# Two heads side by side in the products of an attention pipeline: half the accumulators, one more step of lag

## The chip, the cores and the metric

The kernel runs on one core of a Trainium2 chip. The metric is the device time of one execution in microseconds (us), the median of the runs shown. The engines are TensorE (PE in the profile, with its weight loads as PEld), VectorE (DVE), ScalarE (ACT), GpSimd (POOL) and SyncE (SP, which issues most DMAs).

## What is computed

Two transformer blocks over 512 tokens of width 1024. The first block has two layers of attention with an MLP behind each; the second has attention and a mixture of experts. The change touches the attention of the first block's second layer alone. It has 16 heads in two groups of 8 (a group shares keys and values), head width 64, and three branches whose outputs are gated and added:

```python
def block(args):                       # one block of 128 queries
    i, qb, gb = args
    ...
    p_c = masked_softmax(s_c, cmp_end[None, :] <= t[:, None])    # compressed keys (31 of them)
    o_c = jnp.einsum('bghqn,bngd->bqghd', p_c.astype(vc.dtype), vc)
    ...                                # selection of key blocks
    p_s = masked_softmax(s_s, valid_s[:, :, None]).astype(v_g.dtype)
    o_s = jnp.einsum('bghqk,bgqkd->bqghd', p_s, v_g)             # selected keys
    ...
    p_w = masked_softmax(s_w, valid_w).astype(vw.dtype)
    o_w = jnp.einsum('bghqk,bkgd->bqghd', p_w, vw)               # window
    out = gb[..., 0:1] * o_c + gb[..., 1:2] * o_s + gb[..., 2:3] * o_w
```

With 512 tokens there are 8 blocks of 64 keys and up to 16 may be selected, and the window is 512 wide: the selected and the window branch both attend causally to all keys, each with its own keys and values.

## The kernel before

`layer_1` projects queries, keys and values, makes the compressed keys and their probabilities (`pcT`, transposed and gated), and then runs a software pipeline (`Pipeline`) over items. A step of the pipeline emits one operation of each of several items: an item's operation with lag 5 is emitted five steps after the item's first one. Within a step the order is that of the list `SM1`. Each engine works off its own instructions in the order in which they were emitted, and waits where an operand is not there yet.

An item is one softmax over up to 512 columns: one branch of one head, and one query block of four (`i` = 3, 512 keys) or two (`i` = 2 and 0, or `i` = 1 of both branches). Its operations are `qk` (products with the keys on PE, into a bank of PSUM), `max` (DVE, with the mask), `exp` (ACT), `norm` (the reciprocal on DVE, L618, and the scaling by it and the gate on POOL, L621), `T` (four transposes on PE into another bank, L626), `hi` (the copy of the transposed probabilities to an SBUF tile `PT`, L630, on ACT or DVE in turns), `pv` (the products with the values on PE, L1339) and `out` (the end of a pair of heads). Items come in rounds `f` = 0 to 7, one for each pair of heads, 10 items a round; four more items are for the compressed branch.

The values have 64 columns, so `halves_mm` issues its matmuls in pairs on the two column halves of PE (64 columns each). Before the change the halves are the two branches: the moving operand of a matmul is 256 columns, namely 128 queries of both heads, and the products of four items are emitted together in the step of the fourth. The compressed branch is added by `started`. Two PSUM banks hold the sums of a round; their halves still have to be added together, which `ended` does: for each head and bank a copy of one half by ACT (L1358), and an addition of the other by DVE (L1359) into the SBUF tile `om`; then the split into `oh` (ACT, L1360, rounded to fp32r) and `ol` (DVE, L1361, the rest).

The first nine steps of the pipeline run between the matmuls of the last projection (`q_half(1)`); all others run alone (`attend.run`), but for the last step, which runs within the output projection (`out_proj`, L347).

Of the kernel before, what the change touches and what calls it, by code (L numbers as in the profile page):

```python
# [9 lines left out]
F32 = mybir.dt.float32  # L10
# [3 lines left out]
ALU = mybir.AluOpType  # L14
# [4 lines left out]
S = 512  # L19
# [5 lines left out]
PB = 4  # L25

SM0 = [('pv', 6), ('T', 4), ('max', 1), ('hi', 5), ('norm', 3), ('qk', 0), ('lo', 5), ('out', 7), ('exp', 2)]
SM1 = [('hi', 6), ('norm', 3), ('T', 5), ('max', 1), ('qk', 0), ('exp', 2), ('pv', 7), ('out', 8)]
CM = [('min', 2), ('sm', 3), ('qk', 1), ('out', 6), ('T', 5), ('sc', 0)]
DA = [('qk1', 0), ('hi', 6), ('pv', 7), ('max1', 1), ('T', 5), ('join', 4), ('scale', 3), ('lo', 6), ('exp1', 1)]  # L30
DA0 = [('max0', 1), ('qk0', 0), ('exp0', 2)]
# [55 lines left out]
def tile_kernel(ctx: ExitStack, tc: tile.TileContext, I, out, stage=None, start=None):  # L87
# [11 lines left out]
    def ps(rows=128, cols=512):  # L99
        t = psum.tile([128, 512], F32, tag="ps", name="ps")  # L100
        return t[:rows, :cols]
# [486 lines left out]
    def softmax_item(sched, segs, qk, in1, v, out, ended, gate, parts=None):  # L588


        st = {}
        n = len(segs)
        at, w = [], 0
        for _, i in segs:
            at.append(slice(w, w + (i + 1) * 128))
            w += (i + 1) * 128

        def s_qk():
            st["s"] = ps(128, w)
            qk(st["s"], [(h, i, a) for (h, i), a in zip(segs, at)])  # L600

        def s_max():
            st["nm"] = att.tile([128, 2], F32, tag="nm", name="nm", bufs=4)
            st["p"] = att.tile([128, S], F32, tag="P", name="P", bufs=PBUF)
            for c, ((h, i), a) in enumerate(zip(segs, at)):
                nc.vector.tensor_tensor_reduce(st["p"][:, a], st["s"][:, a], in1(h, i), 1.0, 3e38, ALU.add, ALU.min,  # L606
                                               st["nm"][:, c:c + 1])

        def s_exp():
            st["sm"] = att.tile([128, 2], F32, tag="sm", name="sm", bufs=4)  # L610
            for c, a in enumerate(at):
                p = st["p"][:, a]
                nc.scalar.activation(p, p, AF.Exp, scale=-1.0, bias=st["nm"][:, c:c + 1],  # L613
                                     accum_out=st["sm"][:, c:c + 1])

        def s_norm():
            sm = st["sm"]
            nc.vector.reciprocal(sm[:, :n], sm[:, :n])  # L618
            for c, ((h, i), a) in enumerate(zip(segs, at)):
                p = st["p"][:, a]  # L620
                nc.gpsimd.tensor_scalar(p, p, sm[:, c:c + 1], 1.0 if gate is None else gate(h, i), op0=ALU.mult, op1=ALU.mult)  # L621

        def s_T():
            st["t"] = ps(128, w)
            for j in range(0, w, 128):
                nc.tensor.transpose(st["t"][:, j:j + 128], st["p"][:, j:j + 128], ident)  # L626

        def s_hi():
            if parts:
                (nc.vector.tensor_copy if parts[3] else nc.scalar.copy)(parts[0]()[:, :w], st["t"])  # L630
                return
            st["h"], st["l"] = (att.tile([128, S], F32R, tag="PT" + c, name="PT" + c, bufs=3) for c in "hl")
            nc.scalar.activation(st["h"][:, :w], st["t"], AF.Copy)

        def s_lo():
            if not parts:
                nc.vector.tensor_tensor(st["l"][:, :w], st["t"], st["h"][:, :w], ALU.subtract)

        def s_pv():
            if parts:  # L640
                return parts[1]()
            for (h, i), a in zip(segs, at):
                o, empty, use = out(h)
                pv([(h, i)], [a], o(), v, st["h"], st["l"], empty, use is not None)

        def s_out():
            if parts:
                return parts[2]()
            for h in sorted(ended):
                o, _, use = out(h)  # L650
                if use:
                    use(o())

        fs = dict(pv=s_pv, T=s_T, qk=s_qk, hi=s_hi, max=s_max, exp=s_exp, norm=s_norm, lo=s_lo, out=s_out)
        return [(lag, fs[n]) for n, lag in sched]
# [26 lines left out]
    def lazy(f):  # L682
        box = []

        def get():
            if not box:
                box.append(f())
            return box[0]
        return get
# [151 lines left out]
    def hslice(h):  # L841
        return slice(h % 2 * 64, h % 2 * 64 + 64)
# [247 lines left out]
    def layer_1():  # L1090
# [184 lines left out]
        def scores_T(g, half):  # L1275

            p = ps()
            for h in range(4):
                for n in range(2):
                    nc.tensor.matmul(p, kcs[g][n][:, 96 - h * 32:224 - h * 32], qst[g * 8 + half * 4 + h],  # L1280
                                     start=h == 0 and n == 0, stop=h == 3 and n == 1)
            tag, bufs = ("t4", T4) if g else ("PT", 4)
            scT[g, half] = att.tile([128, S], F32, tag=tag, name="sc", bufs=bufs)
            nc.scalar.activation(scT[g, half], p, AF.Copy)

# [46 lines left out]

        def halves_mm(o, of, start=False, stop=False):
            for c in range(2):
                dst, v, p = of(c)
                nc.tensor.matmul(dst(o[c * 64:c * 64 + 64]), v, p, start=start, stop=stop, skip_group_check=True,  # L1339
                                 tile_position=(0, c * 64))  # L1340

        def started(f):
            o = [ps(), ps()]
            for b in range(2):
                halves_mm(o[b], lambda a: (lambda z: z.rearrange("p (i a n) -> p i a n", i=2, a=2)[:, :, a],
                                           vcs[f // 4][:, f % 2 * 2 + a],
                                           pcT[:, f // 2, b * 256:b * 256 + 256].rearrange("p (i n) -> p i n", i=2)), start=True)
            return o

        def ended(f, o):  # L1350

            y = att.tile([128, S], F32, tag="om", name="om", bufs=1)
            for a in range(2):
                hs = hslice(a)
                for b in range(2):
                    v = o[b].rearrange("p (i a n) -> p i a n", i=2, a=2)[:, :, a]
                    dst = y[hs, b * 256:b * 256 + 256].rearrange("p (i n) -> p i n", i=2)
                    nc.scalar.activation(dst, v[64:128], AF.Copy)  # L1358
                    nc.vector.tensor_tensor(dst, v[0:64], dst, ALU.add)  # L1359
            nc.scalar.activation(oh[:, f], y, AF.Copy)  # L1360
            nc.vector.tensor_tensor(ol[:, f], y, oh[:, f], ALU.subtract)  # L1361

        def qk(s, segs):
            for n, i, a in segs:
# [1 line left out]
                for c in range(2):  # L1366
                    nc.tensor.matmul(s[:, a], qst[h][:, i * 128:w], kst[n % 2][h // 8][c][:, :w], start=c == 0, stop=c == 1)

        def both_pv(i, at, p, o, g):

            for j in range(i + 1):
                halves_mm(o[i // 2], lambda c: (lambda z: z[:, i % 2 * 256:i % 2 * 256 + 256], vsw[:, j, c * 2 + g],
                                                p[c][0][:, :, p[c][1] + at + j * 128:p[c][1] + at + j * 128 + 128]), stop=j == i)

        def pair_items(f):
            o = lazy(lambda: started(f))
            new = lambda: att.tile([128, 2, S], F32, tag="PT", name="PT", bufs=4)
            out = []

            def item(segs, place, take, use, n):  # L1380
                out.append(softmax_item(SM1, segs, qk, lambda n, i: cmask[:, 384 - i * 128:], None, None, None,
                                        lambda n, i: gate[:, i, n // 2 * 3 + 1 + n % 2:n // 2 * 3 + 2 + n % 2],
                                        (place, take, use, n % 2)))
            nothing = lambda: None
            for part in ((3,), (2, 0)):
                p = [lazy(new), lazy(new)]
                for b in range(2):
                    for a in range(2):
                        def take(p=p, part=part):
                            for i, at in zip(part, (0, 384)):  # L1390
                                both_pv(i, at, [(t(), 0) for t in p], o(), f // 4)
                        item([(4 * f + 2 * a + b, i) for i in part], lambda p=p, a=a, b=b: p[b]()[:, a],
                             take if a and b else nothing, nothing, a + b)
            p = lazy(new)
            for a in range(2):
                item([(4 * f + 2 * a, 1), (4 * f + 2 * a + 1, 1)], lambda a=a, p=p: p()[:, a],
                     (lambda p=p: both_pv(1, 0, [(p(), 0), (p(), 256)], o(), f // 4)) if a else nothing,
                     (lambda: ended(f, o())) if a else nothing, a)
            return out

        items = [cmp_item(0, 0), cmp_item(0, 2)]
# [933 lines left out]
```

## Time and profile before

| | |
|---|---|
| median of three runs | 2227.85 us (2227.54 to 2230.63) |
| profiled execution, its own time | 2226.52 us |
| its span in the profile | 2224.8 us |
| mean granted TensorE clock | 0.979 of full speed |
| busy: PE, DVE, ACT, POOL | 95%, 54%, 39%, 20% of the span |

The span runs from the first to the last instruction of the trace; the 1.7 us by which the execution is longer lie around it. Times in the rows below count from the span's start. The steps of the pipeline that run alone lie between some 815 and 977 us.

### The profile page before, as it was taken

The numbers are of one execution on the slowest core, as the hardware profiler recorded it, in microseconds if no ns is written. First come the engines' busy times: TensorE is split into PE (matmuls) and PEld (weight loads), VectorE is DVE, ScalarE is ACT, GpSimd is POOL, SyncE is SP. The second block draws the span as 40 slices with busy tenths as digits, with TensorE's granted clock in tenths as the row PEclk, the third lists the DMA queues.
The fourth block names the chain that finished last, engine by engine and source line by source line (L and its number), as shares of the span: only waits on it lengthen the run. The fifth ranks groups of instructions, "written<-read, shape, count | busy, mean of one in ns | idle before, by whom it ended". The sixth has DMA issues, their size and how long they took to land.

```text
span 2224.8 us, 29271 instructions
## 1 busy us (share of the span) xinstructions
PE 2110.3 (95%) x10935; PEld 1560.8 (70%) x10935; DVE 1192.2 (54%) x2417; ACT 859.4 (39%) x1656; POOL 437.7 (20%) x564
## 2 busy tenths in 40 slices
PE   7999999999999988999999999989888999999997
PEld 6877788888888776668888887777767444444443
DVE  5587654578675557644587686563655132222223
ACT  4524563344343356743344344463653110101000
POOL 4333240000001354531000001454363000000000
PEclk9999999999999999999999999999998999999999
DMA  4221022432313210012532312312016999999995
GB/s 132 68 76 48 1 75 70 160 123 76 114 57 103 84 39 1 1 39 76 170 113 82 119 48 78 102 36 77 29 31 240 372 409 409 409 409 409 409 408 207
DMA packets 118833, 328.62 MB, mean 148 GB/s; under 512 B 10604, under 2 KB 12716, under 8 KB 118688
## 3 DMA queue, kind: packets, MB, share of 16 engines
q1 hardware_dynamic: 115888, 318.87, 39.3%
q0 software_dynamic: 2800, 7.84, 1.1%
q8 instruction: 88, 1.44, 0.3%
q14 instruction: 57, 0.47, 0.1%
HBM read 324.49 MB, written 2.11 MB: 147 GB/s over the span
## 4 chain that ended last, share of the span: by engine, by line
PE 47%; DVE 4%; POOL 1%; ACT 1%; issue 1%; DMA 0%; DVEq 0%; POOLq 0%; ACTq 0%
PE ps L2034 15%; PE ps L404 10%; PE ps L347 8%; PE ps L743 5%; PE ps L2005 3%; PE ps L2101 2%; DVE sl L1740 1%; POOL sh L1736 1%; PE ps L318 0%; POOL wlo L280 0%; DVE w L1724 0%; DVE w L1732 0%; PE ps L319 0%; PE ps L317 0%; PE ps L2052 0%
## 5 line engine op out<-in xcount | busy, mean ns | idle before, releaser
L267 ACT ACTIVATE whi<-raw 128x1024 fp32r<-128x1024 f32 (+2 forms) x162 | 168.3, 1042 | 355.0 <-PE ps L404 153.2
L280 POOL TENSOR_TENSOR wlo<-raw,whi 128x512 fp32r<-128x512 f32 (+1 forms) x132 | 169.1, 1302 | 390.3 <-ACT whi L267 362.0
L2034 PE MATMUL ps<-ew,xt 128*64 128x512 f32 x1024 | 229.9, 597 | 0.0
L282 DVE TENSOR_TENSOR wlo<-raw,whi 128x1024 fp32r<-128x1024 f32 (+2 forms) x96 | 116.7, 1215 | 204.7 <-ACT whi L267 204.4
L404 PE MATMUL ps<-oTl,whi 128*128 128x512 f32 (+2 forms) x576 | 211.4, 371 | 1.4 <-DVE oTl L311 1.4
L404 PE MATMUL ps<-oTh,whi 128*128 128x512 f32 (+2 forms) x576 | 211.6, 371 | 0.5 <-ACT oTh L310 0.5
L404 PE MATMUL ps<-oTh,wlo 128*128 128x512 f32 (+2 forms) x576 | 166.6, 370 | 0.0
L2034 PEld LDWEIGHTS ps<-ew,xt 128*64 128x64 f32 x1024 | 69.4, 137 | 128.2 <-issue 120.1
L347 PE MATMUL ps<-whi,uTh 128*128 128x512 f32 (+2 forms) x384 | 152.6, 398 | 5.0 <-ACT uTh L310 2.9
L347 PE MATMUL ps<-whi,uTl 128*128 128x512 f32 (+2 forms) x384 | 148.5, 388 | 2.9 <-DVE uTl L311 2.9
L347 PE MATMUL ps<-wlo,uTh 128*128 128x512 f32 (+2 forms) x384 | 119.4, 390 | 6.4 <-POOL wlo L280 6.0
L404 PEld LDWEIGHTS ps<-oTl,whi 128*128 128x128 f32 x576 | 108.5, 188 | 20.8 <-DVE oTl L311 2.1
L404 PEld LDWEIGHTS ps<-oTh,whi 128*128 128x128 f32 x576 | 108.5, 188 | 19.8 <-ACT oTh L310 1.2
L2034 PE MATMUL ps<-ew,hid 128*64 128x512 f32 x512 | 118.4, 600 | 0.7 <-ACT hid L2054 0.7
L404 PEld LDWEIGHTS ps<-oTh,wlo 128*128 128x128 f32 x576 | 104.8, 188 | 18.8
L694 DVE TENSOR_TENSOR x<-ps,x 128x512 f32<-128x512 f32 x124 | 82.1, 686 | 66.5 <-PE ps L347 39.6
L445 POOL DMA_DIRECT2D room<-gains x5 | 2.9, 574 | 566.7 <-DVE fwlo L289 283.6
L613 ACT ACTIVATE P<-P,nm 128x512 f32<-128x512 f32 (+2 forms) x192 | 106.0, 554 | 14.0 <-DVE nm L606 13.0
L626 PE MATMUL ps<-cst,P 128*128 128x128 f32 x480 | 79.4, 289 | 22.1 <-POOL P L621 21.6
L2082 POOL CAST pick<-cst 32x128 fp32r<-32x128 f32 x16 | 4.9, 307 | 443.3 <-PE ps L2089 443.3
L2044 ACT ACTIVATE silu<-ps 128x512 f32<-128x512 f32 x16 | 9.6, 597 | 212.8 <-PE ps L2034 212.8
L347 PEld LDWEIGHTS ps<-wlo,uTh 128*128 128x128 f32 x384 | 73.3, 194 | 24.3 <-POOL wlo L280 10.8
(555 smaller groups left out, 5016.8 us busy)
## 6 DMA issues: line engine op xcount, KB each, us to landing
ew<-w SPq DMA_DIRECT2D x384, 512.0 KB, 10.2
raw<-mlp_w SPq DMA_DIRECT2D x80, 512.0 KB, 3.6
fraw<-mlp_w SPq DMA_DIRECT2D x48, 512.0 KB, 5.8
raw<-w_in SPq DMA_DIRECT2D x24, 512.0 KB, 3.9
raw<-ab_w_in SPq DMA_DIRECT2D x20, 512.0 KB, 3.5
raw<-c_w_in SPq DMA_DIRECT2D x12, 512.0 KB, 3.5
raw<-ab_w_out SPq DMA_DIRECT2D x8, 512.0 KB, 3.7
raw<-c_w_out SPq DMA_DIRECT2D x8, 512.0 KB, 3.7
```

What stands on the lines that cost most here:

```text
L267: nc.scalar.activation(hi[:, :w], raw[:, :w], AF.Copy)
L280: nc.gpsimd.tensor_tensor(lo[:, h], raws[r][:, h], hi[:, h], ALU.subtract)
L282: nc.vector.tensor_tensor(lo[:, :w], raws[r][:, :w], hi[:, :w], ALU.subtract)
L347: nc.tensor.matmul(p, a[:, tt], w[:, k], start=u == 0 and n == 0, stop=u == nk - 2 and n == 5)
L404: nc.tensor.matmul(p[:, tt], w[:, k, ff], b[:, u + k, tt], start=start and n == 0, stop=u == nk - 2 and n == 5, **kw)
L613: nc.scalar.activation(p, p, AF.Exp, scale=-1.0, bias=st["nm"][:, c:c + 1], accum_out=st["sm"][:, c:c + 1])
L626: nc.tensor.transpose(st["t"][:, j:j + 128], st["p"][:, j:j + 128], ident)
L694: nc.vector.tensor_tensor(xs, p, xs, ALU.add)
L743: nc.tensor.matmul(acc[b][t], p[:, 2 * h + k, tt], v[:, k], start=begins and h == 0 and m == 0, stop=m == 5, skip_group_check=True)
L2005: nc.tensor.matmul(v, htok[a][:, t, c * 128:(c + 1) * 128], oo[q][:, t], start=t == 0 and a == 0, stop=t == NT - 1 and a == 1)
L2034: nc.tensor.matmul(p[n][half(b)], xs[:, half(b)], w[b][:, n * 512:n * 512 + 512], start=k == 0, stop=k == nk - 1)
L2101: nc.tensor.matmul(p, ot[r][:, t * 128:(t + 1) * 128], ys[r][a][:, nn], start=j == 0 and a == 0, stop=j == len(rs) - 1 and a == 1)
```

## The change

- The two column halves are the two heads of the round, not the two branches. A matmul's moving operand is 128 queries of one head, so `both_pv` issues two pairs (one for each branch) of 128 columns where there was one pair of 256. The branches are added up by accumulation in one PSUM bank; `started` writes the compressed branch with one pair of 512 columns.
- `ended` has one ACT copy from that bank into `oh` and one DVE subtraction from that bank into `ol`; the tile `om` goes.
- An item pair (two heads, one branch) has its products two items earlier than the four together had: `take` is called at every second item.
- `PT` tiles are [128, 512], eight of them, where four of [128, 2, 512] were.
- In `SM1` the lag of `hi` is 7 (6 before), of `pv` 8 (7), of `out` 9 (8).

```diff
-SM1 = [('hi', 6), ('norm', 3), ('T', 5), ('max', 1), ('qk', 0), ('exp', 2), ('pv', 7), ('out', 8)]
+SM1 = [('hi', 7), ('norm', 3), ('T', 5), ('max', 1), ('qk', 0), ('exp', 2), ('pv', 8), ('out', 9)]
...
-        def halves_mm(o, of, start=False, stop=False):
+        def halves_mm(o, at, of, start=False, stop=False):
             for c in range(2):
-                dst, v, p = of(c)
-                nc.tensor.matmul(dst(o[c * 64:c * 64 + 64]), v, p, start=start, stop=stop, skip_group_check=True,
+                nc.tensor.matmul(o[c * 64:c * 64 + 64, at], *of(c), start=start, stop=stop, skip_group_check=True,
                                  tile_position=(0, c * 64))
...
         def started(f):
-            o = [ps(), ps()]
-            for b in range(2):
-                halves_mm(o[b], lambda a: (lambda z: z.rearrange("p (i a n) -> p i a n", i=2, a=2)[:, :, a],
-                                           vcs[f // 4][:, f % 2 * 2 + a],
-                                           pcT[:, f // 2, b * 256:b * 256 + 256].rearrange("p (i n) -> p i n", i=2)), start=True)
+            o = ps()
+            halves_mm(o, slice(0, S), lambda a: (vcs[f // 4][:, f % 2 * 2 + a], pcT[:, f // 2, :]), start=True)
             return o
...
         def ended(f, o):
-            y = att.tile([128, S], F32, tag="om", name="om", bufs=1)
-            for a in range(2):
-                hs = hslice(a)
-                for b in range(2):
-                    v = o[b].rearrange("p (i a n) -> p i a n", i=2, a=2)[:, :, a]
-                    dst = y[hs, b * 256:b * 256 + 256].rearrange("p (i n) -> p i n", i=2)
-                    nc.scalar.activation(dst, v[64:128], AF.Copy)
-                    nc.vector.tensor_tensor(dst, v[0:64], dst, ALU.add)
-            nc.scalar.activation(oh[:, f], y, AF.Copy)
-            nc.vector.tensor_tensor(ol[:, f], y, oh[:, f], ALU.subtract)
+            nc.scalar.activation(oh[:, f], o, AF.Copy)
+            nc.vector.tensor_tensor(ol[:, f], o, oh[:, f], ALU.subtract)
...
-        def both_pv(i, at, p, o, g):
+        def both_pv(i, at, b, p, o, g):
             for j in range(i + 1):
-                halves_mm(o[i // 2], lambda c: (lambda z: z[:, i % 2 * 256:i % 2 * 256 + 256], vsw[:, j, c * 2 + g],
-                                                p[c][0][:, :, p[c][1] + at + j * 128:p[c][1] + at + j * 128 + 128]), stop=j == i)
+                halves_mm(o, slice(i * 128, i * 128 + 128),
+                          lambda c: (vsw[:, j, b * 2 + g], p[c]()[:, at + j * 128:at + j * 128 + 128]), stop=j == i)
...
+            new = lambda: att.tile([128, S], F32, tag="PT", name="PT", bufs=8)
...
+            def items(segs, take, use=nothing):
+                p = [lazy(new), lazy(new)]
+                for a in range(2):
+                    out.append(softmax_item(SM1, segs(a), qk, lambda n, i: cmask[:, 384 - i * 128:], None, None, None,
+                                            lambda n, i: gate[:, i, n // 2 * 3 + 1 + n % 2:n // 2 * 3 + 2 + n % 2],
+                                            (p[a], (lambda: take(p)) if a else nothing, use if a else nothing, a)))
             for part in ((3,), (2, 0)):
                 for b in range(2):
+                    def take(p, part=part, b=b):
+                        for i, at in zip(part, (0, 384)):
+                            both_pv(i, at, b, p, o(), f // 4)
+                    items(lambda a, b=b, part=part: [(4 * f + 2 * a + b, i) for i in part], take)
+
+            def last(p):
+                for b in range(2):
+                    both_pv(1, 256 * b, b, p, o(), f // 4)
+            items(lambda a: [(4 * f + 2 * a, 1), (4 * f + 2 * a + 1, 1)], last, lambda: ended(f, o()))
```

## Rows read from the trace of the kernel before

**Rows 1.** The page: busy shares, and the chain by engine

```profile
PE 2110.3 (95%) x10935; PEld 1560.8 (70%) x10935; DVE 1192.2 (54%) x2417; ACT 859.4 (39%) x1656; POOL 437.7 (20%) x564
...
PE 47%; DVE 4%; POOL 1%; ACT 1%; issue 1%; DMA 0%; DVEq 0%; POOLq 0%; ACTq 0%
```

**Rows 2.** Busy us by stretch: length, PE PEld DVE ACT POOL; PEclk, DMA, GB/s

```profile
820.00:980.00 160.00, 142.65 (x990) 106.03 (x990) 106.45 (x408) 107.50 (x325) 76.27 (x126) 0.93 0.00 1
```

**Rows 3.** PE's waits from 822 to 872 us: in total, times, longest

```profile
PE ps L626 <- POOL P L621: 3.4, 2, 2.1
```

**Rows 4.** PE's waits from 884 to 970 us

```profile
PE ps L626 <- POOL P L621: 10.5, 5, 2.1
```

**Rows 5.** Timeline at the end of round 3: start, length (us), engine, instruction [idle before]

```profile
902.25 0.62 PE L626 MATMUL ps<-cst,P 128*128 128x128 f32 x4
...
903.33 1.08 PE L1339 MATMUL ps<-PT,vsw 128*64 128x256 f32 x8
...
904.35 0.66 PE L626 MATMUL ps<-cst,P 128*128 128x128 f32 x4
...
904.51 0.65 ACT L1358 ACTIVATE om<-ps 64x256 f32<-64x256 f32 x2
...
904.92 1.61 DVE L1359 TENSOR_TENSOR om<-ps,om 64x256 f32<-64x256 f32 x4 [0.23 <-ACT om L1358]
...
905.36 0.62 PE L626 MATMUL ps<-cst,P 128*128 128x128 f32 x4
...
906.30 0.60 PE L626 MATMUL ps<-cst,P 128*128 128x128 f32 x4
906.57 0.63 ACT L1360 ACTIVATE oTh<-om 128x512 fp32r<-128x512 f32 x1 [0.48 <-DVE om L1359]
...
907.23 0.69 DVE L1361 TENSOR_TENSOR oTl<-om,oTh 128x512 fp32r<-128x512 f32 x1 [0.70 <-ACT oTh L1360]
...
907.84 0.68 DVE L630 COPY PT<-ps 128x512 f32<-128x512 f32 x1
...
908.44 0.15 DVE L618 RECIPROCAL sm<-sm 128x2 f32<-128x2 f32 x1
...
908.79 1.73 POOL L621 TENSOR_SCALAR P<-P,sm,gate 128x384 f32<-128x384 f32 x3 [3.52 <-ACT PT L630]
...
909.51 0.86 PE L626 MATMUL ps<-cst,P 128*128 128x128 f32 x4 [2.13 <-POOL P L621]
```

**Rows 6.** Busy us by stretch, columns as in rows 2: where the clock was low, and one where not

```profile
863.00:866.40 3.40, 3.40 (x12) 2.32 (x12) 1.32 (x6) 1.45 (x6) 2.52 (x5) 0.61 0.00 0
...
890.40:893.60 3.20, 3.20 (x17) 2.29 (x18) 2.82 (x13) 3.20 (x13) 3.02 (x7) 0.60 0.01 3
894.00:907.00 13.00, 13.00 (x105) 10.33 (x102) 8.03 (x31) 8.35 (x24) 5.61 (x9) 1.00 0.01 2
910.90:914.10 3.20, 3.20 (x19) 1.77 (x20) 1.66 (x6) 2.57 (x10) 2.21 (x5) 0.60 0.00 0
...
931.40:934.50 3.10, 3.10 (x18) 1.58 (x14) 0.64 (x2) 1.54 (x6) 1.19 (x3) 0.59 0.00 0
...
969.00:972.00 3.00, 3.00 (x18) 1.49 (x15) 0.00 (x0) 0.60 (x4) 1.07 (x2) 0.59 0.00 0
```

**Rows 7.** Timeline: the products of four items, two records a matmul

```profile
899.36 1.95 PE L1339 MATMUL ps<-PT,vsw 128*64 128x256 f32 x16
```

**Rows 8.** Groups of instructions, 820 to 980 us: count, busy us, mean ns, idle before

```profile
L626 PE MATMUL ps<-cst,P 128*128 128x128 f32 x303 | 50.5, 289 | 16.4 <-POOL P L621 15.9
L1339 PE MATMUL ps<-PT,vsw 128*64 128x256 f32 x320 | 42.3, 407 | 0.0
...
L1339 PEld LDWEIGHTS ps<-PT,vsw 128*64 128x64 f32 x320 | 23.2, 146 | 12.9 <-issue 3.7
...
L1359 DVE TENSOR_TENSOR om<-ps,om 64x256 f32<-64x256 f32 x32 | 12.0, 412 | 4.9 <-ACT om L1358 4.0
...
L1358 ACT ACTIVATE om<-ps 64x256 f32<-64x256 f32 x32 | 10.9, 377 | 5.7 <-PE ps L1339 3.9 <-DVE om L1359 1.7
```

More of the change, by code (lines that the diff above doesn't have):

```diff
@@ L1281, in scores_T @@
                                      start=h == 0 and n == 0, stop=h == 3 and n == 1)
-            tag, bufs = ("t4", T4) if g else ("PT", 4)
+            tag, bufs = ("t4", T4) if g else ("PT", 8)
             scT[g, half] = att.tile([128, S], F32, tag=tag, name="sc", bufs=bufs)
@@ L1375, in pair_items @@
         def pair_items(f):
             o = lazy(lambda: started(f))
-            new = lambda: att.tile([128, 2, S], F32, tag="PT", name="PT", bufs=4)
+            new = lambda: att.tile([128, S], F32, tag="PT", name="PT", bufs=8)
             out = []
[L1380 to L1383, printed above, removed]
@@ L1385, in pair_items @@
             for part in ((3,), (2, 0)):
-                p = [lazy(new), lazy(new)]
                 for b in range(2):
[L1388 to L1398, printed above, removed]
+                    def take(p, part=part, b=b):
+                        for i, at in zip(part, (0, 384)):
+                            both_pv(i, at, b, p, o(), f // 4)
```

## The prediction

> **What bounds the kernel now.** Read the page first: PE is busy for 95% of the span, and the chain that ended last lies almost wholly on it [rows 1]. So only what PE does, or waits for, can move the time much; DVE and ACT count where PE waits for them. Next the stretch in which the pipeline runs alone [rows 2]. Of 160 us PE is busy for 142.65 at a mean granted clock of 0.93, DVE for 106.45, ACT for 107.50, POOL for 76.27; DMA does nothing. No engine is full there, so one looks for who holds up whom. PE's waits name one holder: the transposes L626 wait for POOL's scaling L621, twice between 822 and 872 us, 3.4 us in all, and five times between 884 and 970, 10.5 us [rows 3, 4]. That is seven waits, one for each of the rounds 0 to 6; the eighth round ends under the output projection.
>
> The timeline around one of them shows why [rows 5]. At 904.35 the products of the round are issued and the next transposes start. ACT copies halves of the banks from 904.51 on, DVE adds four times, ACT rounds at 906.57, and DVE's subtraction runs from 907.23 to 907.92. All of this is one chain to and fro between two engines in order, and behind it in DVE's queue stand a copy of PT (907.84) and a reciprocal (908.44). POOL, idle for 3.52 us, scales at 908.79, PE transposes at 909.51. Meanwhile PE had three short steps, with no products in them: transposes at 904.35, 905.36 and 906.30, 0.94 to 1.01 us a step, done about 907.3. The chain from 904.35 to 909.51 is 5.16 us long, the work that covers it about 3: PE stands for 2.13 us.
>
> The clock is the second cost. In five stretches of 3.0 to 3.4 us the granted clock averages 0.59 to 0.61, so 1.2 GHz most of the time, with PE busy throughout; the 13 us from 894 on, without a wait, are at 1.00 [rows 6]. Each of the five comes right behind one of the seven waits (two waits have none).
>
> **The change part by part.**
>
> *The end of a round.* Eight instructions of ACT and DVE on 64x256 go (four of 377 ns, four of 412 ns [rows 8]); the rounding and the subtraction stay (0.63 and 0.69 us [rows 5]), both now from PSUM. For the rounding from PSUM there is no row with this output; I take the 0.63. The chain behind the last product becomes 0.63 + 0.69 + 0.68 (copy of PT) + 0.15 (reciprocal) + 0.72 (scaling, 908.79 to 909.51), and about 0.6 for three handovers like the 0.2 from 908.59 to 908.79: 3.5 us instead of 5.16. Even under the old cover of 3 us PE would stand for 0.5 us, not 2.13.
>
> *Products at every second item.* The cover grows as well. Now the step after next behind a round's end holds the first products of the next round and its compressed branch: to the three steps (2.9 us) come eight records on two halves (0.88 us), the compressed branch (as much), and a switch (0.25, below): 4.9 us. The chain of 3.5 us is covered, and 1.4 us are to spare. So all seven waits go: -13.9 us (3.4 + 10.5). The least that this part can bring is seven times (2.13 - 0.5), some 11 us.
>
> *The clock behind the waits.* The five stretches are 15.9 us long; at full clock their work takes 0.6 of that: -6.4 us. If the clock stays as it is, 0; if the edges outside my stretches count, -8.
>
> *The products themselves.* A matmul is two records on each half. Eight pairs of records take 1.95 us [rows 7]; the last lasts 0.41, so a pair of 256 columns comes every (1.95 - 0.41) / 7 = 0.22 us. There are 160 pairs before (320 records [rows 8]) and 320 of 128 columns after. The nearest row for 128 columns is the transposes, four in 0.60 to 0.62 us with 0.29 for the last, so one every 0.11 us, its own weight load included [rows 5, 8]. Half of 0.22 is 0.11: the pairs cost as much together as before, 0. From above: if PE waited for the whole load of 146 ns [rows 8] with every pair, 320 x 0.036 = +12 us. I take 0, because the transposes load twice as many columns in the same 0.11. The compressed branch is one pair of 512 columns for two of 256: 0.
>
> *Switches between forms.* PE goes to its halves five times a round, not three times. A step with four pairs lasts from 902.25 to 904.35, 2.10 us; without products 0.97; four pairs are 0.88 [rows 5]. The rest, 0.25 us, is the price of going there and back. 8 rounds x 2 x 0.25 = +4.0 us. From below 0, if it hides. The Trainium skill, TensorEngine Tiling (Array Packing), Key Properties, speaks against the change here: changing the tiling mode drains the engine. The 0.25 us agree; without that rule the sum would be 4.0 us lower.
>
> *Copies and products a step later.* The copies stand first in ACT's and DVE's steps, so with a lag of 7 they no longer hold up the exponentials behind them until PE's transposes of one step before. The transposed bank is held one step longer, but the sums hold one bank instead of two: PSUM stays even. The eight PT tiles are as large together as the four. 0 in the sum. The pipeline has one step more; at its drain no instruction is added, the last products come behind the same last transposes, with 0.9 us of other products between: 0, at worst +1. No DMA and no POOL instruction is added, moved or passed by another.
>
> *Is there another bound behind PE?* With 16 us less, DVE has 106.45 - 12.0 and ACT 107.50 - 10.9 in 144 us [rows 2, 8]: 66 and 67%. No.
>
> **The sum.** -13.9 - 6.4 + 4.0 = -16.3 us. Against the profiled execution, 2226.52: 2210.2. The median of the runs is 1.3 above it, so I forecast 2211.5. What comes after is issued behind this stage and moves with it.
>
> **The rivals.**
>
> 1. *The clock does not recover* although the waits go. Of seven waits two were not followed by a low stretch, and long stretches without waits are at 1.00 [rows 6], so rather no. -13.9 + 4.0: 2218.
>
> 2. *Short pairs wait for their weights.* Twice as many loads for the same columns: +12, so 2223.7. Against it the transposes. The Trainium skill, TensorE: Matmul & The Clock Gate, Back-to-back issue gap, gives about 81 ns at 128 columns and 131 at 512 for bf16 streams of loads and matmuls, so few columns cost more each; the rows here (0.11 against 0.22) don't show it for fp32.
>
> 3. *PE keeps waiting at the round's end*, because the recurrence has another cause: DVE's reciprocal or the copies, now elsewhere in the order, are late again, and the clock falls behind it. Half the waits and no clock: -7 + 4.0, 2224.5.
>
> 4. *The two halves stop running side by side* with 128 columns, say for want of issue or because both heads load the same values: each pair takes 0.11 more. 320 x 0.11 = +35: 2246, slower. It decides from 16.3 / 320 = 0.05 us a pair on. Against it: a pair of 256 columns comes every 0.22 us, twice the 0.11 of a single transpose of 128, so the halves do run side by side before [rows 7], and nothing that made them is taken away.
>
> 5. *More than the sum*: the switches hide (-4.0) and the clock gives 8: 2206.
>
> **How the numbers follow.** What differs by under 0.2% (4.5 us) can hardly be told from no change. Chances: the forecast 0.58 (2208 to 2216), rival 1 0.13, rival 2 0.08, rival 3 0.08, rival 4 0.05, rival 5 0.08. Rivals 2 and 3 lie at the edge of what can be told (2223.4): half of their 0.16 counts as the same. Faster: 0.58 + 0.13 + 0.08 + 0.08 = 0.87; same 0.08; slower 0.05. The range runs from the gain of rival 5 with 2 us on its far side (2204) to rival 2 (2224); it leaves out rival 4 and parts of 2, 3 and 5.
>
> **What the profile after would show.** PE's transposes without the seven waits of 2 us; 640 records of 128 columns with a pair every 0.11 us; a mean clock of 0.98 or more in this stretch; the stretch of [rows 2] some 16 us shorter; one ACT and one DVE instruction at a round's end. Wrong would be: waits of PE for POOL as long as before, pairs at 0.15 us or more, low stretches without waits, or a new wait of PE for a PSUM bank (copies that come a step later free it later).

## The result, and the profile after

The changed kernel takes 2206.4 us (median of four runs, 2203.8 to 2209.3) where the kernel before takes 2229.2 beside it: ratio 0.9898, 95% interval 0.9881 to 0.9915, or 22.8 us less (19 to 27). Forecast were 2211.5 us, 16.3 less, in a range of 2204 to 2224, and faster with a chance of 0.87. The direction and the places are right; the size of two terms and the reason given for one are not.

The profiled execution took 2207.28 us. Its page, busy shares and the chain that ended last, to be held against [rows 1]:

```profile
PE 2105.7 (95%) x11223; PEld 1568.5 (71%) x11223; DVE 1179.3 (53%) x2385; ACT 847.9 (38%) x1624; POOL 439.1 (20%) x564
...
PE 55%; DVE 5%; POOL 2%; ACT 1%; issue 1%; DMA 0%; DVEq 0%; POOLq 0%; ACTq 0%
```

PE is about as busy in all, in 19 us less, and the chain still lies on it. The stretch from the first transpose behind the pipeline's fill to the output projection, in the kernel before and in the changed one (busy us by stretch: length, PE PEld DVE ACT POOL; PEclk, DMA, GB/s):

```profile
819.50:977.40 157.90, 140.54 (x980) 104.39 (x980) 105.45 (x405) 106.28 (x322) 76.65 (x127) 0.93 0.00 1
```

```profile
819.60:956.20 136.60, 134.28 (x1269) 110.94 (x1269) 94.50 (x378) 96.11 (x294) 77.35 (x128) 0.98 0.01 2
```

The stretch is 21.3 us shorter, which is the whole gain: it starts at the same time, and what lies behind it takes 1249.3 us instead of 1247.4 (between 1247 and 1252 in all profiles here but that of the experiment that works on other numbers). PE stands for 2.3 us in it (its length less PE's busy time), where it stood for 17.4. PE's waits of the changed kernel from 820 to 958 us, and from 878 to 957 alone:

```profile
PE ps L626 <- POOL P L621: 4.7, 2, 4.5
PE ps L1321 <- POOL cx L1315: 1.9, 2, 1.6
```

```profile
PE ps L626 <- POOL P L621: 0.2, 1, 0.2
```

The 4.5 us are the fill, just ahead of the stretch: the projection has ended, and the first softmaxes are not ready. The seven waits of [rows 3, 4] are gone, all of them (the first had been 1.26 us long, the others 1.99 to 2.14); what is left belongs to the items of the compressed branch. The end of round 3 after the change, to be held against [rows 5] (timeline):

```profile
896.59 1.09 PE L1337 MATMUL ps<-PT,vsw 128*64 128x128 f32 x16
...
897.61 0.66 PE L626 MATMUL ps<-cst,P 128*128 128x128 f32 x4
897.73 0.60 ACT L1346 ACTIVATE oTh<-ps 128x512 fp32r<-128x512 f32 x1 [0.15 <-PE ps L1337]
...
898.22 0.58 ACT L630 COPY PT<-ps 128x512 f32<-128x512 f32 x1
898.36 0.69 DVE L1347 TENSOR_TENSOR oTl<-ps,oTh 128x512 fp32r<-128x512 f32 x1 [0.41 <-ACT oTh L1346]
...
898.58 0.60 PE L626 MATMUL ps<-cst,P 128*128 128x128 f32 x4
...
898.97 0.16 DVE L618 RECIPROCAL sm<-sm 128x2 f32<-128x2 f32 x1
...
899.29 1.10 POOL L621 TENSOR_SCALAR P<-P,sm,gate 128x384 f32<-128x384 f32 x2 [0.75 <-DVE sm L618]
```

From the round's last products (897.61) to POOL's scaling it is 1.7 us; before it was 4.4 (904.35 to 908.79). The reader is to see one thing that the prediction missed: the copy of PT in this place is now ACT's (898.22), not DVE's, and no longer stands in front of the reciprocal. The line that the diff changes for it looks harmless: the last argument of an item was `a + b` and is `a`, and by its parity ACT or DVE copies. So before the change the copies were not strictly in turns: four items had ACT, DVE, DVE, ACT.

### The profile page after: what moved, and what is told of

Its sections match the earlier page's. It is cut to its first block, busy times and chain, and to the rows that moved or that the text cites. A ratio compares the mean times of both kernels' runs of the same rounds, so it can differ in the third digit from the quotient of the medians.

```text
span 2205.5 us, 29775 instructions
## 1 busy us (share of the span) xinstructions
PE 2105.7 (95%) x11223; PEld 1568.5 (71%) x11223; DVE 1179.3 (53%) x2385; ACT 847.9 (38%) x1624; POOL 439.1 (20%) x564
## 4 chain that ended last, share of the span: by engine, by line
PE 55%; DVE 5%; POOL 2%; ACT 1%; issue 1%; DMA 0%; DVEq 0%; POOLq 0%; ACTq 0%
PE ps L2019 16%; PE ps L404 10%; PE ps L347 8%; PE ps L743 5%; PE ps L1990 3%; PE ps L2086 2%; PE ps L1337 2%; PE ps L626 2%; PE ps L1353 2%; DVE sl L1725 1%; POOL wlo L280 1%; PE ps L318 1%; POOL sh L1721 1%; PE ps L319 0%; PE ps L317 0%
## 5 line engine op out<-in xcount | busy, mean ns | idle before, releaser
L606 DVE CUSTOM_DVE_ANT_0 P<-ps,cst 128x128 f32<-128x128 f32 (+3 forms) x168 | 75.0, 473 | 37.5 <-POOL P L621 19.1
```

## The experiments

Theory 1 is the prediction's: PE waits by what the chain at a round's end exceeds the work that covers it, and the clock falls behind such waits. Rival 2: the short end alone does it. Rival 3: the later copies do it. (These numbers are those of the expectations, not those of the prediction's rivals.) All kernels are compared by the stretch of above, which one profile of each shows, and by time.

**The lags alone, in the kernel before.**

```diff
-SM1 = [('hi', 6), ('norm', 3), ('T', 5), ('max', 1), ('qk', 0), ('exp', 2), ('pv', 7), ('out', 8)]
+SM1 = [('hi', 7), ('norm', 3), ('T', 5), ('max', 1), ('qk', 0), ('exp', 2), ('pv', 8), ('out', 9)]
```

> The kernel before with nothing but the three lags one step longer (copies 7, products 8, end 9). Measure: the stretch from the first transpose after the pipeline's fill to the output projection alone, 157.9 us before and 136.5 us after the change. Theory 1 (a round's end is a chain of ACT and DVE, 5.2 us long before and 3.5 after; PE waits by what it exceeds the work that covers it, 2.9 us with the products of four items together, 4.9 with those of two): the chain and its cover are those of before, so the seven waits of about 2 us stay; stretch 156 to 160, time as before within 3 us. Rival 2 (the shorter chain alone brings all, cover counts for nothing): the same. Rival 3 (the later copies free ACT and DVE of PE's transposes, and that brings it): the waits go, stretch about 140, 17 us faster.

Ratio 0.9975 (0.9958 to 0.9992), stretch 153.2 us; the ten runs spread from 2214.2 to 2226.8 us, and the profile is that of the longest. Its PE's waits from 822 to 975 us (the fill's 4.5 is the longest of them):

```profile
PE ps L626 <- POOL P L621: 15.0, 6, 4.5
```

Five waits of 10.5 us in all stay at the rounds' ends, so rival 3 falls. But two of seven, those of the first rounds, are gone, and the stretch is 4.7 us shorter; theory 1 had 156 to 160 us, so this is a miss for theory 1 as well. Why the first alone, stays open.

**The lags of before, in the changed kernel**, the same line the other way round.

> The changed kernel with the three lags of before (6, 7, 8). Theory 1: chain 3.5 us, cover 4.9 us as in the changed kernel; no waits at the rounds' ends, stretch 136 to 139 us, within 3 us of the changed kernel. Rival 2: the same. Rival 3: the copies stand in front of the exponentials again, most of the waits come back, stretch 148 or more, at least 12 us slower than the changed kernel.

Ratio 0.9918 (0.9890 to 0.9946), stretch 134.4 us (820.9 to 955.3). Here 1.3 us of products run ahead of the fill's wait and so outside the stretch, which makes about 135.7 us against 136.6. No wait at a round's end. The lags are not needed.

**The products of four items together, in the changed kernel.** The short end stays; only the cover of the chain is that of before.

```diff
+                held = []
                 for b in range(2):
-                    def take(p, part=part, b=b):
-                        for i, at in zip(part, (0, 384)):
-                            both_pv(i, at, b, p, o(), f // 4)
+                    def take(p, part=part, b=b, held=held):
+                        held.append(p)
+                        if b:
+                            for i, at in zip(part, (0, 384)):
+                                for c in range(2):
+                                    both_pv(i, at, c, held[c], o(), f // 4)
```

> The changed kernel, but the products of four items are issued together in the step of the fourth, as before the change; the end of a round stays short. Theory 1: chain 3.5 us against a cover of 2.9: seven waits of about 0.5 us (+3.5), 16 switches of 0.22 fewer (-3.5); stretch 135 to 140 us. Rival 2: no waits, only the switches go, stretch 133 us. Rival 3: the same as rival 2.

Ratio 0.9902 (0.9877 to 0.9928). PE's waits from 820 to 954 us, and the stretch:

```profile
PE ps L626 <- POOL P L621: 4.5, 1, 4.5
PE ps L1321 <- POOL cx L1315: 2.4, 1, 2.4
```

```profile
819.70:953.60 133.90, 131.28 (x1269) 113.34 (x1269) 93.66 (x378) 94.71 (x294) 77.17 (x127) 0.97 0.01 2
```

The waits of 0.5 us that theory 1 expected are not there. Rival 2's number (133) fits better: the issue at every second item is not what removed the waits.

**The long end, in the changed kernel.**

```diff
+            y = att.tile([128, S], F32, tag="om", name="om", bufs=1)
+            for a in range(2):
+                hs = hslice(a)
+                for b in range(2):
+                    v = o[hs, b * 256:b * 256 + 256]
+                    dst = y[hs, b * 256:b * 256 + 256]
+                    nc.scalar.activation(dst, v, AF.Copy)
+                    nc.vector.tensor_tensor(dst, v, dst, ALU.max)
-            nc.scalar.activation(oh[:, f], o, AF.Copy)
-            nc.vector.tensor_tensor(ol[:, f], o, oh[:, f], ALU.subtract)
+            nc.scalar.activation(oh[:, f], y, AF.Copy)
+            nc.vector.tensor_tensor(ol[:, f], y, oh[:, f], ALU.subtract)
```

> The changed kernel with the long end of a round put back: four ACT copies and four DVE operations on 64x256 in turns (the operation is a maximum of a value with itself, so nothing is left out of the result), then the rounding and the subtraction from that tile. Theory 1: chain 5.2 us against a cover of 4.9: seven waits of at most 0.3 us, stretch 137 to 141 us, 0 to 5 us slower than the changed kernel. Rival 2: the waits and the low clock behind them come back, stretch 152 or more, 16 us or more slower. Rival 3: no difference.

Ratio 0.9966 (0.9952 to 0.9980), 13 to 15 us of the gain gone (the profile is that of the longest of ten runs, 2225.3 us, their median 2220.2). The stretch, PE's waits from 822 to 971 us, and the end of a round:

```profile
821.60:971.30 149.70, 138.95 (x1268) 112.10 (x1268) 106.34 (x406) 106.81 (x322) 77.15 (x127) 0.96 0.01 2
```

```profile
PE ps L626 <- POOL P L621: 12.4, 6, 4.5
```

```profile
881.91 0.66 PE L626 MATMUL ps<-cst,P 128*128 128x128 f32 x4
...
888.69 1.11 PE L626 MATMUL ps<-cst,P 128*128 128x128 f32 x4 [3.68 <-POOL P L621]
...
906.60 0.66 PE L626 MATMUL ps<-cst,P 128*128 128x128 f32 x4
...
906.71 0.38 ACT L1352 ACTIVATE om<-ps 64x256 f32<-64x256 f32 x1 [0.15 <-PE ps L1337]
907.12 0.42 DVE L1353 TENSOR_TENSOR om<-ps,om 64x256 f32<-64x256 f32 x1 [0.19 <-ACT om L1352]
...
907.58 0.38 ACT L1352 ACTIVATE om<-ps 64x256 f32<-64x256 f32 x1 [0.48 <-DVE om L1353]
907.99 0.42 DVE L1353 TENSOR_TENSOR om<-ps,om 64x256 f32<-64x256 f32 x1 [0.44 <-ACT om L1352]
...
911.46 0.16 DVE L618 RECIPROCAL sm<-sm 128x2 f32<-128x2 f32 x1
...
912.50 0.76 PE L626 MATMUL ps<-cst,P 128*128 128x128 f32 x4 [0.95 <-POOL P L621]
```

Theory 1's 137 to 141 us were missed; rival 2's 152 or more lie nearer. Besides the fill, five waits of 7.9 us in all stand at the rounds' ends: 3.68 us at the end of round 2, three times 0.95, and 1.41 at the last of them.

One reason is that the end put back is longer than the old one. ACT and DVE read from one bank in strict turns, 0.87 us for each of four (907.12 to 907.99), while before they worked on two banks and overlapped; that the one bank is the reason is argued, not shown. So the chain is 5.9 us (906.60 to 912.50) and not 5.2. The cover that the prediction worked out was 4.9; chain minus cover gives 1.0, and three waits are 0.95. The other reason the theory left out: at the end of round 2 no products and no compressed branch lie in the three steps that cover the chain. There the chain is 6.8 us (881.91 to 888.69) and the cover 3.1 (881.91 to 888.69 - 3.68 = 885.01). So the products at every second item do cover some 2 us more, though not at every round's end; only the short end has no use for it.

**The short end alone, in the kernel before.** It leaves out the adding up of the halves and the second bank. What follows then works on other numbers (PE has 208 more matmuls, none of them in the stretch, and the total is 2277.5 us), so the stretch alone is read.

```diff
-            y = att.tile([128, S], F32, tag="om", name="om", bufs=1)
...
-            nc.scalar.activation(oh[:, f], y, AF.Copy)
-            nc.vector.tensor_tensor(ol[:, f], y, oh[:, f], ALU.subtract)
+            nc.scalar.activation(oh[:, f], o[0], AF.Copy)
+            nc.vector.tensor_tensor(ol[:, f], o[0], oh[:, f], ALU.subtract)
```

> The kernel before with the short end alone: a round's end is one ACT rounding and one DVE subtraction from the first of the two banks. This leaves out the adding up of the halves and the second bank. Products, lags, banks and copies as before. Theory 1 (wait = chain minus cover): chain 2.5 us and 0.7 more where DVE's copy of the probabilities stands in front of the reciprocal, 3.2 us in all, cover 2.9: seven waits of about 0.3 us instead of 2.1, no stretch of low clock behind them; stretch 157.9 - 13 - 8 = 135 to 141 us. Rival (the new column halves, the bank that comes free or the lags bring much of it): stretch 145 or more.

```profile
817.00:952.70 135.70, 132.21 (x980) 99.99 (x980) 95.43 (x377) 96.19 (x294) 76.62 (x127) 0.98 0.01 1
```

```profile
893.22 0.66 PE L626 MATMUL ps<-cst,P 128*128 128x128 f32 x4
...
894.57 0.68 DVE L630 COPY PT<-ps 128x512 f32<-128x512 f32 x1
...
895.17 0.15 DVE L618 RECIPROCAL sm<-sm 128x2 f32<-128x2 f32 x1
...
895.52 1.09 POOL L621 TENSOR_SCALAR P<-P,sm,gate 128x384 f32<-128x384 f32 x2 [1.37 <-ACT PT L630]
...
896.24 0.44 PE L626 MATMUL ps<-cst,P 128*128 128x128 f32 x2
```

The first fence is the stretch, the second a round's end. The stretch falls by 22.2 us, a little more than with the whole change (21.3). All seven waits are gone with the old products, the old lags, two banks and the copy of 894.57 still in front of the reciprocal. The chain with that copy is 3.0 us (893.22 to 896.24), and the old cover of about 3.0 (904.35 to 909.51 - 2.13 = 907.38 in [rows 5]) just holds it. So the short end is the cause; where nothing is left out, it is the adding up in one bank that makes it possible.

**The engines of the copies.** Twice: in the changed kernel with four products together, copies in the old order (the parity of `a + b`); and in the kernel before, copies in turns (`a`).

```diff
-                                            (p[a], (lambda: take(p)) if a else nothing, use if a else nothing, a)))
+                                            (p[a], (lambda: take(p)) if a else nothing, use if a else nothing, (a + b) % 2)))
```

```diff
-                             take if a and b else nothing, nothing, a + b)
+                             take if a and b else nothing, nothing, a)
```

> The changed kernel with the products of four items together, and the copies of the probabilities given to ACT and DVE in the order of before (ACT, DVE, DVE, ACT in four items, not in turns). Theory 1: DVE's copy is again in front of the reciprocal behind a round's end, the chain is 0.7 us longer (3.2 against a cover of 2.8): waits of 0.2 to 0.5 us at the rounds' ends, stretch 135 to 138 us against 133.9 in turns. Rival (which engine copies is of no account): no waits, 133 to 135 us.

> The kernel before, with the copies of the probabilities given to ACT and DVE in turns, as the changed kernel does. Theory 1: the chain at a round's end loses DVE's copy of 0.68 us: the waits fall from 2.13 to about 1.45 us, the stretch from 157.9 to 153, and less if the clock holds behind shorter waits (down to 145). Rival: the waits stay at 2.1 us, stretch 156 to 160.

The first: ratio 0.9909 (0.9893 to 0.9926), stretch 135.5 us, no wait at a round's end but one of 0.5 us in the drain; PE's waits L626 on POOL are 0.7 us in all. The copy does add to the chain, but a chain of 3.0 us is still covered; theory 1's waits of 0.2 to 0.5 us are a miss. The second: ratio 0.9959 (0.9945 to 0.9973). Its stretch, a wait, and two stretches of its clock:

```profile
818.90:965.40 146.50, 133.59 (x980) 102.02 (x980) 103.60 (x404) 105.05 (x321) 76.62 (x127) 0.97 0.01 1
```

```profile
905.48 0.76 PE L626 MATMUL ps<-cst,P 128*128 128x128 f32 x4 [1.53 <-POOL P L621]
```

```profile
886.40:889.80 3.40, 3.40 (x18) 2.90 (x18) 3.32 (x16) 3.40 (x15) 3.19 (x6) 0.62 0.01 2
906.00:921.00 15.00, 15.00 (x118) 11.64 (x117) 10.51 (x44) 11.40 (x35) 8.43 (x14) 1.00 0.01 2
```

One argument is worth 9 us. Six of the seven waits are 0.6 us shorter, as expected (five are 1.53 us instead of 2.13, the first 0.66 instead of 1.26); and behind waits of 1.53 us the clock stayed at 1.00. The seventh, at 884.8, is still 1.98 us long, and behind it the clock fell (0.62). Lost to the clock were 157.9 x 0.07 = 11.1 us before and are 146.5 x 0.03 = 4.4, 6.7 less. PE's idle time is 4.5 us less (17.4 to 12.9). That makes 11.2 of the 11.4 us.

**Versions that the runs point to.** Four products together and the old lags; and that, as well as the changed kernel, with 12 steps of the pipeline instead of 9 between the matmuls of the last projection, against the wait of the fill.

```diff
-        q_half(1, fine=after(FS, *turns, *[attend.step] * QF1))
+        two = lambda: (attend.step(), attend.step())
+        q_half(1, fine=after(FS, *turns, *[attend.step] * 8, two, two))
```

> The changed kernel with the products of four items together and the lags of before (6, 7, 8). Theory 1: a short end with the copy on ACT is covered whatever the lags, so no waits at the rounds' ends, and 16 switches fewer than in the changed kernel: stretch 132 to 135 us, at least as fast as the changed kernel. Rival (with the products together the lags are needed): waits of 0.5 us and more at the rounds' ends, stretch 137 us or more.

> The version with the products of four items together and the lags of before, with 12 steps of the pipeline instead of 9 between the matmuls of the last projection (the last two of its ten slots take two steps each). What is left of waits after the change is the pipeline's fill: 5.67 us in this version, 4.5 in the changed kernel, with 6.8 us of low clock behind it. Theory 1 (PE waits only where POOL's scaling is late against the steps that cover it): three more steps have their softmax behind them when the projection ends, the fill wait falls by 2 to 4 us, time 2 to 6 us under the version without it, so about 2202 where the changed kernel has 2206. Rival: the projection has four of the eight PSUM banks until its end, so the added steps wait for banks there and give back what they gain: no difference.

> The changed kernel with the same 12 steps within the last projection. With its lags a transposed bank is held one step longer, so PSUM is tighter while the projection has four banks. Theory 1: fill wait 4.5 us down to 2 to 3, time 1 to 4 us under the changed kernel. Rival: PE waits for banks within the projection and the time is that of the changed kernel or above.

The first: 0.9911 (0.9894 to 0.9927), and no wait at a round's end, as expected. Its stretch:

```profile
820.10:953.30 133.20, 130.59 (x1268) 111.22 (x1268) 93.33 (x376) 94.94 (x293) 76.61 (x127) 0.98 0.01 2
```

The second: 2204.3 us, ratio 0.9896 (0.9879 to 0.9912); the third: 2206.2, 0.9903 (0.9886 to 0.9919). The fill's wait of 5.67 us is gone in the second, as these waits of PE from 780 to 956 us show, but 3.4 us of others, for DVE's stacking of the queries, stand in its place:

```profile
PE ps L1182 <- DVE stk L1174: 3.4, 4, 1.4
PE ps L626 <- POOL P L621: 1.3, 1, 1.3
PE ps L1182 <- DVE rb L533: 1.2, 1, 1.2
PE ps L1321 <- POOL cx L1315: 0.8, 1, 0.8
```

The third had been expected 1 to 4 us under the changed kernel and is not. The second version has the lowest median, 2 us under the changed kernel, the least that was expected of it, and the intervals of all of these overlap: a better version than the changed kernel is not shown.

## Why the prediction was right, and where it was off

The stretch went from 157.9 to 136.6 us, -21.3, where the sum had -16.3.

*The seven waits: -13.9 forecast, -15.0 measured* (PE's idle time 17.4 to 2.3 us). Right, the other 1.1 us being a wait of the drain (the pipeline's last steps; 0.7 us before) and parts of the compressed items'. What failed is the step that explains it, "the end of a round". It made the chain 3.5 us, so that the old cover would leave a wait of 0.5, and it needed the products at every second item to cover it. The chain with the copy is 3.0 us, since the engines hand over in less than the 0.6 us allowed. Without the copy, as in the changed kernel, it is 2.4: POOL starts at 899.29 and needs 0.72 for the first part (as in [rows 5], 908.79 to 909.51), which ends 2.4 us behind 897.61. Neither chain needed the products at every second item or the later copies. The "least" of 11 us for the short end was too low: it brings all. That the number came out all the same is luck in part: a chain taken too long was set against a cover that was not needed.

*The clock: -6.4 forecast.* The low stretches behind the waits are gone, that at the fill stays. From the mean clocks of the two stretches: 157.9 x 0.07 = 11.1 us lost before, 136.6 x 0.02 = 2.7 after, -8.3. The mechanism was right, the term mis-sized: my stretches of [rows 6] cut the edges, and the forecast named 8 as the other bound.

*Switches between forms: +4.0.* Measured by the kernel with four products together, which has 16 fewer: its stretch is 2.7 us shorter, though its clock lost 1.3 us more and PE stood 0.3 us longer. 16 switches are some 4.3 us, 0.27 each; 0.25 was taken. With the old lags besides, at a mean clock of 0.98 as in the changed kernel, PE's busy time is 3.7 us less (130.59 against 134.28). So the products at every second item cost PE some 4 us, for nothing in return. The runs do not tell it: their medians are 2206.4 with these products and 2205.1 and 2206.4 without.

*The products themselves: 0.* Sixteen records of 128 columns take 1.09 us, the last 0.28, so one pair every (1.09 - 0.28) / 7 = 0.12 us, against 0.22 for 256 columns. From their start to the next transposes, eight pairs take 1.02 us (896.59 to 897.61), as four pairs of 256 columns did (903.33 to 904.35). Rivals 2 and 4 fall; the transposes were the right row to go by. That few columns cost more each, as the Trainium skill, TensorE: Matmul & The Clock Gate, Back-to-back issue gap, has it for bf16, hardly shows here.

*Copies a step later: 0.* Needed for nothing with the short end (about 135.7 us with the old lags); alone they were worth 4.7 us of the stretch, unforeseen.

*Sum.* -15.0 - 8.3 + 4.3 = -19.0; 2.3 us of the 21.3 are not accounted for. No run shows where these come from. Rival 1 (the clock does not recover) and rival 3 (waits stay, by another cause) did not come. Rival 5, 2206, is the nearest number, by its clock term and not by its switches. (By its own terms rival 3 comes to 2224.9, not 2224.5; nothing hangs on it.)

## What to carry to other kernels

Where an engine waits at a regular place, measure two lengths from the same event: the chain that leads to the instruction it waits for, through every queue in order, and the work it has meanwhile. The wait is the difference, so either can be changed, and only one has to be: here the chain, and the second remedy cost PE some 4 us of switches. Work out the cover for every place, not for one: with the long end put back it was 3.1 us at the end of round 2 and about 4.9 at others. Look then for strangers in the queues of the chain: one copy of 0.68 us that could go to the other engine, at no cost in instructions, was worth 9 us in the kernel before. And count the clock with the wait: shortening waits of 2.1 to 1.5 us gained more through the clock (6.7 us) than through the waits (4.5).

## What the runs showed of the hardware that was not expected

Behind idle times of PE of 0.95 and 1.53 us in this pipeline the granted clock stayed at 2.4 GHz; behind those of 1.98 us and more it mostly fell to 1.2 GHz (in 13 of 15 cases in the stretches of all kernels above, the fill apart). But the length of one idle time does not settle it. In the kernel with the lags alone the clock also fell once behind 1.39 us, as its timeline and its clock (columns as in rows 2) show:

```profile
887.03 0.76 PE L626 MATMUL ps<-cst,P 128*128 128x128 f32 x4 [1.39 <-POOL P L621]
```

```profile
888.60:891.90 3.30, 3.30 (x14) 2.26 (x12) 2.92 (x15) 3.30 (x14) 3.11 (x7) 0.50 0.00 0
```

ACT and DVE reading one PSUM bank took 0.87 us for a copy and an operation on 64x256, always one waiting for the other; on two banks they overlapped. The trace names the other engine's instruction as what ended each wait (0.44 and 0.48 us in the rows of the long end); whether the chip or the program asks for the turns is not shown.
